# Hybrid decoder block on one core: the output projection in slab pairs with seven-product multiplication, and a new order of steps in all slab pairs

## The chip, the core and the metric

The kernel runs on one core of one Trainium2 chip. The metric is the device time in microseconds. An execution of the kernel before takes 1348.54 us, the median of 3 runs (1348.43 to 1349.02).

## The reference

All values are float32, 256 tokens of width 2048. After an RMSNorm one large projection feeds two attention branches and two sets of gates; then

```python
mixed = g_a * (y_a @ w_branch_a[l]) + g_b * (y_b @ w_branch_b[l])
h = h + mixed @ w_out[l]                                   # 2048 x 2048

hn = rmsnorm(h, ffn_norm[l])
h = h + (jax.nn.silu(hn @ w_gate[l]) * (hn @ w_up[l])) @ w_down[l]   # 2048 x 5632 twice, 5632 x 2048
return rmsnorm(h, final_norm)
```

The change touches this last part, from `mixed` on.

## The kernel before, in words

**Products in three passes.** Each float32 operand is split into a high part in the type float32r and the low rest. A product is hi*hi + lo*hi + hi*lo, all summed in one PSUM accumulator. Activations (128 rows each of two row blocks t = 0, 1) are the stationary operand, weights the moving one, 512 columns wide. A weight tile `raw` (4 times 128 rows by 512 columns, 1 MB) arrives by a DMA that SP issues (`load`, line 904). Six such tiles exist, four of one pool and two of another. `split` (line 916) makes from half a tile the high part `wh` on ScalarE (line 927) and the low part `wl` on VectorE (line 928), each 128 x 1024. It frees the tile after its last use and issues the next load.

**Steps.** All work is written out by hand as a list of steps, and the loop at line 1003 walks it. A plain step takes half a weight tile against both row blocks: 12 matmuls (line 1026 for the passes with `wh`, line 1031 for the pass with `wl`, which comes last). At step s the split of step s + 3 is issued first (`AHEAD`, with four buffers each of `wh` and `wl`), then whatever was put off to this step with `later(d, fn)` or `at(job, d, fn)`, then the step's matmuls. Every engine works through its own queue in the order of issue.

**Jobs.** A job takes one slab of 512 output columns over all chunks of 512 rows of the weight; a plain job of w_out has 8 steps. A pair takes two slabs at once (`pair_steps`, line 832): gate and up columns together for 11 pairs gu0 to gu10, two w_down slabs together for dn0 and dn1. Here the tiles are named (x, c): slab x = 0 or 1 (a and b in the change), chunk c. In two chunks r0, r1 and two slabs the pair replaces eight block products by seven (Winograd's form), each of two steps of 6 matmuls. With A11, A12 the first row block of the two chunks and A21, A22 the second:

- VectorE changes the four weight tiles in place by four subtractions (line 843): T1 = (1, r0) - (0, r0); T2 = (1, r1) - T1; T3 = T2 - (0, r0); T4 = (0, r1) - T2. Each is 128 x 2048 and is issued as `pre` of a split, ahead of its cast.
- The activations give row sums (`row_sums`, line 221): S1 = A21 + A22, S2 = S1 - A11, S3 = A11 - A21, S4 = A12 - S2, four additions on VectorE, then two casts and two subtractions for their high and low parts.
- P1 = A11 (0, r0), P2 = A12 (0, r1), P3 = S4 (1, r1), P4 = A22 T4, P5 = S1 T1, P6 = S2 T2, P7 = S3 T3. They go to four accumulators "11", "21", "12", "22" (row block, slab); all four PSUM buffers of that pool are in use by one pair. `alone` (line 678) copies four intermediate states to SBUF tiles A and B.

In the kernel before the two chunks are 0 and 1 for every pair, and a pair's 22 steps are P1, a20, P5, P2, a22, P3, P6, a30, P4, P7, a32, then b20, b22, b30, b32 (a20: slab a, chunk 2, first half; each P is two steps). T1 goes ahead of P1, T2 of P2, T3 of P3, T4 of P6. The other chunks of w_down follow as plain steps.

**Around the pairs.** `cut` (line 214) splits a transposed chunk into high and low parts. In w_out's jobs, `wout_done` (line 638) adds an accumulator to the residual `xt`, sums its squares on ScalarE (line 166), scales the rows to `hr` (line 654), has TensorE transpose them (line 207), and cuts them: chunk c of the next operand `hop`. The row sums of `hop` are made after slab 1, in the w_out stage. In a gu pair, `gate` (line 691) empties "11" and "21" and applies Silu near the end of the pair; `up` (line 698) empties "12" and "22" in the first step of the next one, with four VectorE operations; the result is transposed in that next pair's fourth and fifth step. `feed` and `feed_sums` (lines 980 to 990) cut the chunks for w_down and make its row sums, once for each of dn0 and dn1, around the start of dn0 and dn1.

## Time and profile before

| what | value |
|---|---|
| median of 3 runs | 1348.54 us |
| the profiled execution | 1348.63 us |
| its span, first to last instruction | 1346.8 us |
| mean granted TensorE clock | 0.943 of full |
| w_out stage in the trace | about 513 to 607 us |
| gu0 to gu10 | 607 to 1083 us |
| dn0, dn1 | 1083 to 1210, 1210 to 1337 us |

The profile is of one execution. Busy times are by engine: PE is TensorE's matmuls, DVE VectorE, ACT ScalarE, SP the engine that issues the loads. A timeline row gives start, duration, engine, line, output <- inputs, and how many instructions were merged; in brackets stands idle time before it and what ended it. Ends of matmuls are modelled.

### The profile page before, as it was taken

How to read it: one execution, taken by the hardware profiler on the slowest of the kernel's cores; microseconds unless marked ns; L12 is line 12 of the kernel's file. 1: busy time of each engine (PE TensorE's matmuls, PEld its weight loads, DVE VectorE, ACT ScalarE, POOL GpSimd, SP SyncE). 2: the span in 40 equal slices, each digit the busy share in tenths (PEclk: the TensorE clock that was granted, in tenths of full speed). 3: DMA queues.
4: the chain of work that ended last, by engine and by line, in shares of the span. 5: the costliest groups of instructions: out<-in, count | busy, mean ns of one | idle time of the engine just before them, and what ended most of it. 6: DMA issues, size and time to landing. Idle time of an engine off the chain costs nothing.

```text
span 1346.8 us, 15873 instructions
## 1 busy us (share of the span) xinstructions
PE 1305.4 (97%) x5990; PEld 1081.8 (80%) x5990; DVE 993.2 (74%) x1212; ACT 782.8 (58%) x1000; POOL 2.1 (0%) x11
## 2 busy tenths in 40 slices
PE   8999999999999999998999999999999989998997
PEld 6888888888888888776887878778787868886885
DVE  5766667674565565578888998889888997579654
ACT  6455555654444454656666666667666665446553
POOL 0000000000000000000000000000000000000000
PEclk9999999999999999999999999999999989998998
DMA  8565544455555565543557545674457637553731
GB/s 295 187 205 182 164 159 153 160 174 189 187 183 160 190 244 188 188 157 118 173 209 250 191 151 185 223 249 156 159 186 249 220 124 250 190 185 108 267 125 63
DMA packets 126969, 249.06 MB, mean 185 GB/s; under 512 B 4486, under 2 KB 9132, under 8 KB 126892
## 3 DMA queue, kind: packets, MB, share of 16 engines
q1 hardware_dynamic: 126620, 247.78, 54.8%
q8 instruction: 47, 0.77, 0.2%
q10 hardware_dynamic: 272, 0.26, 0.1%
q14 instruction: 30, 0.25, 0.1%
HBM read 245.93 MB, written 2.10 MB: 184 GB/s over the span
## 4 chain that ended last, share of the span: by engine, by line
PE 92%; DVE 5%; ACT 2%; issue 1%; DMA 0%; ACTq 0%; SPq 0%; DVEq 0%
PE acc L1026 58%; PE acc L1031 29%; DVE wl L928 2%; DVE raw L843 1%; PE aT_tp L207 1%; ACT wh L927 1%; PE sb L435 1%; ACT junk L166 1%; PE ya L471 0%; PE yb L471 0%; DMA x<-in_x_dram 0%; PE sa L435 0%; PE hT_tp L207 0%; PE xT_tp L183 0%; ACT hr L654 0%
## 5 line engine op out<-in xcount | busy, mean ns | idle before, releaser
L928 DVE TENSOR_TENSOR wl<-raw,wh 128x1024 fp32r<-128x1024 f32 (+2 forms) x546 | 649.2, 1211 | 289.7 <-ACT wh L927 265.8
L927 ACT CAST wh<-raw 128x1024 fp32r<-128x1024 f32 (+2 forms) x546 | 568.1, 1044 | 406.0 <-PE acc L1026 359.6
L1026 PE MATMUL acc<-wh,xh 128*128 128x512 f32 (+1 forms) x512 | 139.4, 394 | 0.0
L1026 PE MATMUL acc<-wh,xl 128*128 128x512 f32 (+1 forms) x512 | 135.5, 387 | 0.0
L1031 PE MATMUL acc<-wl,xh 128*128 128x512 f32 (+1 forms) x512 | 135.3, 386 | 0.0
L843 DVE TENSOR_TENSOR raw<-raw,raw 128x2048 f32<-128x2048 f32 x52 | 118.8, 2285 | 0.4
L1026 PEld LDWEIGHTS acc<-wh,xl 128*128 128x128 f32 x512 | 95.7, 189 | 19.7
L1031 PEld LDWEIGHTS acc<-wl,xh 128*128 128x128 f32 x512 | 95.7, 189 | 19.3
L1026 PEld LDWEIGHTS acc<-wh,xh 128*128 128x128 f32 x512 | 92.0, 190 | 15.2
L1026 PE MATMUL acc<-wh,h2h 128*128 128x512 f32 x176 | 47.1, 390 | 0.0
L1031 PE MATMUL acc<-wl,h2h 128*128 128x512 f32 x176 | 47.1, 389 | 0.0
L1026 PE MATMUL acc<-wh,h3h 128*128 128x512 f32 x176 | 47.1, 389 | 0.0
L1026 PE MATMUL acc<-wh,h2l 128*128 128x512 f32 x176 | 47.0, 389 | 0.0
L1026 PE MATMUL acc<-wh,h3l 128*128 128x512 f32 x176 | 47.0, 389 | 0.0
L1031 PE MATMUL acc<-wl,h3h 128*128 128x512 f32 x176 | 47.0, 389 | 0.0
L1026 PEld LDWEIGHTS acc<-wh,h3h 128*128 128x128 f32 x176 | 33.0, 188 | 6.9
L1031 PEld LDWEIGHTS acc<-wl,h2h 128*128 128x128 f32 x176 | 33.0, 188 | 6.9
L1026 PEld LDWEIGHTS acc<-wh,h3l 128*128 128x128 f32 x176 | 33.0, 188 | 6.9
L1026 PEld LDWEIGHTS acc<-wh,h2l 128*128 128x128 f32 x176 | 33.0, 188 | 6.9
L1031 PEld LDWEIGHTS acc<-wl,h3h 128*128 128x128 f32 x176 | 33.0, 188 | 6.9
L1026 PEld LDWEIGHTS acc<-wh,h2h 128*128 128x128 f32 x176 | 33.0, 188 | 6.8
L1031 PE MATMUL acc<-wl,hq0h 128*128 128x512 f32 x88 | 28.5, 405 | 9.4 <-DVE wl L928 9.4
(444 smaller groups left out, 2013.8 us busy)
## 6 DMA issues: line engine op xcount, KB each, us to landing
raw<-in_w_in_dram SPq DMA_DIRECT2D x59, 1024.0 KB, 5.1
raw<-in_w_gate_dram SPq DMA_DIRECT2D x44, 1024.0 KB, 6.9
raw<-in_w_up_dram SPq DMA_DIRECT2D x44, 1024.0 KB, 5.3
raw<-in_w_down_dram SPq DMA_DIRECT2D x44, 1024.0 KB, 5.2
...
```

The source lines that it names most:

```text
L166: nc.scalar.activation(junk[:, :src.shape[-1]], src, AF.Square, accum_out=acc)
L207: nc.tensor.transpose(tp[:, k, t * P:(t + 1) * P], nat[:, t, (j + k) * P:(j + k + 1) * P], ident)
L435: nc.tensor.matmul(ps[:, t, :], lhsT=l, rhs=r, start=i == 0, stop=i == len(mm) - 1)
L843: sub = lambda o, x, y: (lambda: nc.vector.tensor_sub(raws[G[o]], raws[G[x]], raws[G[y]]))
L927: nc.scalar.copy(hi, v)
L928: nc.vector.tensor_sub(lo, v, f32(hi))
L1026: nc.tensor.matmul(accs[key], lhsT=lhs(k)[i], rhs=hi[:, k], start=i == 0 and k == 0 and jb["first"][key] == s, stop=False, skip_group_chec ...
L1031: nc.tensor.matmul(accs[key], lhsT=lhs(k)[0], rhs=lo[:, k], start=False, stop=(st["read"] or jb["last"][key] == s) and k == 1, skip_group_ ...
```

## The change

The four jobs of w_out become two pairs, wo0 and wo1, each with seven products. The order of a pair's steps is now given by a text, one word per step or product: PLAIN_FIRST for wo0 and gu0, BETWEEN for wo1 and gu1 to gu10, DOWN for dn0 and dn1. The seven products use chunks 2 and 3 (w_out, gate/up) or 3 and 4 (w_down). T2 and T3 are both issued ahead of P6's first half, T4 ahead of its second half. The transposed chunks 2 and 3 of `mixed` are copied to SBUF and cut, and their row sums made; those of `hop` are made from chunks 2 and 3, in gu0; those of w_down's operand once, in dn0, and kept with the cuts of chunks 3 and 4 for dn1. The put-off distances of the residual's leaving change, the Sqrt is issued one step after its inputs, and the multiplication by the final gains is one operation, three steps later.

```diff
+PLAIN_FIRST = "a00 a02 a10 a12 1 2 5 6 3 4 7 b00 b02 b10 b12"
+BETWEEN = "1 a00 2 5 a02 6 3 a10 4 7 a12 b00 b02 b10 b12"
+DOWN = "a00 a02 a10 a12 a20 a22 1 2 a50 5 6 a52 3 4 7 b00 b02 b10 b12 b20 b22 b50 b52"
...
-            nc.scalar.activation(t, v, AF.Sqrt)
+            if apart:
+                later(1, lambda: nc.scalar.activation(t, v, AF.Sqrt))
+            else:
+                nc.scalar.activation(t, v, AF.Sqrt)
...
-            mh.append(big([P, 4, S], f"mh{c}", F32R))
-            ml.append(big([P, 4, S], f"ml{c}", F32R))
-            spread(2, b, mh[c], ml[c], f"mT{c}")
+            if c >= 2:
+                mF[c] = big([P, 4, S], f"mF{c}")
+                for i in range(2):
+                    later(2 + i, lambda i=i: turned(b, mF[c], f"mT{c}", 2 * i))
+
+                def ready():
+                    mop[c] = cut(mF[c], f"m{c}")
+                    if c == 3:
+                        mop["s"], add, finish = row_sums(mF[2], mF[3], "m")
+                        later(1, add)
+                        later(2, finish)
+                later(4, ready)
+            else:
+                mop[c] = [big([P, 4, S], f"m{c}{x}", F32R) for x in "hl"]
+                spread(2, b, *mop[c], f"mT{c}")
...
-    def wout_done(c):
-
-        def done(ps):
...
+    def h_leaves(c, ps, keys):
+
+        h = xt[c]
+        for t in range(NT):
+            nc.vector.tensor_add(h[:, t], ps[keys[t]], h[:, t])
+            sumsq(h[:, t], ssh[:, t, c:c + 1])
+        d, e = ((8, 4), (8, 4), (1, 2), (1, 1))[c]
+        if c == 0:
+            later(2, h0_root)
+            later(5, h0_invert)
+        st = {}
...
-                nc.vector.tensor_add(h[:, t], ps[t], h[:, t])
-                sumsq(h[:, t], ssh[:, t, c:c + 1])
-            d = 4 if c == 0 else 1
-            if c == 0:
-                later(1, h0_root)
-                later(3, h0_invert)
-            st = {}
...
-            def ready():
-                hop[c] = cut(hF[c], f"h{c}")
-                if c == 1:
-                    hop["s"], add, finish = row_sums(hF[0], hF[1], "h")
-                    later(1, add)
-                    later(2, finish)
-            later(d, rows)
-            for i in range(2):
-                later(d + 1 + i, lambda i=i: turned(st["n"], hF[c], f"hT{c}", 2 * i, "ffn", 4 * c))
-            later(d + 3, ready)
...
+        def ready():
+            hop[c] = cut(hF[c], f"h{c}")
             if c == 3:
-                later(3, h_root)
-                later(5, h_invert)
-
-                def both():
-                    v = L["h0_v"]
-                    nc.vector.tensor_mul(hs, v, R["h0"])
-                    nc.vector.tensor_mul(hs, hs, R["h"])
-                later(6, both)
-        return done
+                hop["s"], add, finish = row_sums(hF[2], hF[3], "h")
+                later(1, add)
+                later(2, finish)
+        later(d, rows)
+        for i in range(2):
+            later(d + e + i, lambda i=i: turned(st["n"], hF[c], f"hT{c}", 2 * i, "ffn", 4 * c))
+        later(d + e + 2, ready)
+        if c == 3:
+            later(1, h_root)
+            later(4, h_invert)
+
+            def both():
+                nc.vector.tensor_mul(hs, L["h0_v"], R["h0"])
+                nc.vector.tensor_mul(hs, hs, R["h"])
+            later(5, both)
...
+    def to_residual(jb, j, name):
+
+        A, B = big([P, NT, 512], f"{name}A{j}"), big([P, NT, 512], f"{name}B{j}")
+        alone(jb, A, B)
+        for i, x in enumerate((A, B)):
+            later(jb["pos"]["P7"] + 1 + i, lambda i=i, x=x: nc.vector.tensor_add(xt[2 * j + i], xt[2 * j + i], x))
+
+    def wout_begin(j):
+        def begin(jb):
+            ps, pos = jb["accs"], jb["pos"]
+            to_residual(jb, j, "wo")
+            later(pos["a"] + 1, lambda: h_leaves(2 * j, ps, ("11", "21")))
+            later(pos["b"], lambda: h_leaves(2 * j + 1, ps, ("12", "22")))
+        return begin
...
-            A, B = big([P, NT, 512], f"dA{j}"), big([P, NT, 512], f"dB{j}")
-            alone(jb, A, B)
-            for i, x in enumerate((A, B)):
-                later(pos["P7"] + 3 + i, lambda i=i, x=x: nc.vector.tensor_add(xt[2 * j + i], xt[2 * j + i], x))
+            to_residual(jb, j, "dn")
...
             def leave(i):
                 h = xt[2 * j + i]
                 for t in range(NT):
                     nc.vector.tensor_add(h[:, t], ps[("11", "21", "12", "22")[2 * i + t]], h[:, t])
                     sumsq(h[:, t], ssf[:, t, 2 * j + i:2 * j + i + 1])
-                    nc.vector.tensor_mul(h[:, t], h[:, t], L["gf"][j][:, i])
+                later(3, lambda: nc.vector.tensor_mul(h, h, L["gf"][j][:, i, None, :].to_broadcast([P, NT, 512])))
             if j == 0:
                 later(pos["a"], lambda: leave(0))
                 later(pos["b"], lambda: leave(1))
...
-    for c in range(4):
-        job(w_out[:, 512 * c:512 * (c + 1)], 16, lhs_of(mh, ml), wout_done(c), f"wo{c}")
+    slabs = lambda w, j: [w[:, 512 * c:512 * (c + 1)] for c in (2 * j, 2 * j + 1)]
+    for j in range(2):
+        pair(slabs(w_out, j), 16, mop, wout_begin(j), f"wo{j}", (2, 3), (PLAIN_FIRST, BETWEEN)[j])
     for c in range(11):
-        pair((w_gate[:, 512 * c:512 * (c + 1)], w_up[:, 512 * c:512 * (c + 1)]), 16, hop, gu_begin(c), f"gu{c}")
+        pair((w_gate[:, 512 * c:512 * (c + 1)], w_up[:, 512 * c:512 * (c + 1)]), 16, hop, gu_begin(c), f"gu{c}",
+             (2, 3), BETWEEN if c else PLAIN_FIRST)
     for j in range(2):
-        pair([w_down[:, 512 * c:512 * (c + 1)] for c in (2 * j, 2 * j + 1)], 44, aop, dn_begin(j), f"dn{j}")
+        pair(slabs(w_down, j), 44, aop, dn_begin(j), f"dn{j}", (3, 4), DOWN)
...
-        wa, wb = jb["w"]
+        order = jb["order"].split()
+        r0, r1 = jb["region"]
+        done = max([r1] + [int(u[1]) for u in order if u[0] in "ab"]) + 1
+        for u in order:
+            for x, c in {"1": ((0, r0), (1, r0)), "2": ((0, r1), (1, r1))}.get(u, (("ab".find(u[0]), int(u[-2:-1] or 0)),)):
+                if x >= 0:
+                    get(x, c)
+        for c in range(done, n):
+            get(0, c)
+            get(1, c)
...
-        get((0, 0), (1, 0), (0, 2), (0, 1), (1, 1), (0, 3), (1, 2), (1, 3), *[(x, c) for c in range(4, n) for x in range(2)])
-
-        def seven(name, key, src, lhs, pre=None):
-            for k0 in (0, 2):
-                add_step(jb, G[src], k0, [(key, lhs(k0))], pre if k0 == 0 else None, name)
+        def seven(name, key, src, lhs, *pre):
+            for k0, before in zip((0, 2), (*pre, None, None)):
+                add_step(jb, G[src], k0, [(key, lhs(k0))], before, name)
...
-        seven("P1", "22", (0, 0), A(0, 0), sub((1, 0), (1, 0), (0, 0)))
-        eight(0, 2, 0)
-        seven("P5", "12", (1, 0), S_(1))
-        seven("P2", "11", (0, 1), A(1, 0), sub((1, 0), (1, 1), (1, 0)))
-        eight(0, 2, 2)
-        seven("P3", "12", (1, 1), S_(4), sub((0, 0), (1, 0), (0, 0)))
-        seven("P6", "22", (1, 0), S_(2), sub((0, 1), (0, 1), (1, 0)))
-        eight(0, 3, 0)
-        seven("P4", "21", (0, 1), A(1, 1))
-        seven("P7", "22", (0, 0), S_(3))
-        eight(0, 3, 2, "a")
-        for c in (2, 3):
-            for k0 in (0, 2):
-                eight(1, c, k0, "b")
-        for c in range(4, n):
+        T1, T2 = sub((1, r0), (1, r0), (0, r0)), sub((1, r0), (1, r1), (1, r0))
+        T3, T4 = sub((0, r0), (1, r0), (0, r0)), sub((0, r1), (0, r1), (1, r0))
+        products = {"1": ("22", (0, r0), A(r0, 0), T1), "2": ("11", (0, r1), A(r1, 0)), "5": ("12", (1, r0), S_(1)),
+                    "6": ("22", (1, r0), S_(2), lambda: (T2(), T3()), T4), "3": ("12", (1, r1), S_(4)),
+                    "4": ("21", (0, r1), A(r1, 1)), "7": ("22", (0, r0), S_(3))}
+        for u in order:
+            if u in products:
+                seven("P" + u, *products[u])
+            else:
+                eight("ab".index(u[0]), int(u[1]), int(u[2]), u[0])
+        for c in range(done, n):
             for x, k0 in ((0, 0), (0, 2), (1, 0), (1, 2)) if c == n - 1 else ((0, 0), (1, 0), (0, 2), (1, 2)):
                 eight(x, c, k0, "ab"[x])
+        jb["pos"]["a"] = max(jb["pos"][u] for u in ("a", "P2", "P4", "P7"))
...
-    def feed_sums(j):
-        def go():
-            aop["s"], add, finish = row_sums(aF[0], aF[1], f"d{j}")
-            add()
-            later(2, finish)
-        return go
+    def feed_sums():
+        aop["s"], add, finish = row_sums(aF[3], aF[4], "d")
+        add()
+        later(2, finish)
 
     for j in range(2):
-        at(f"dn{j}", -6, feed(j, 0))
-        at(f"dn{j}", -5, feed_sums(j))
-        at(f"dn{j}", -2, feed(j, 2))
-        at(f"dn{j}", -1, feed(j, 1))
-        at(f"dn{j}", 8, feed(j, 3))
-        for c in range(4, 11):
-            at(f"dn{j}", 22 + 4 * (c - 4) - 4, feed(j, c))
-    at("dn0", 0, load_gfin)
+        at(f"dn{j}", -4, feed(j, 0))
+        at(f"dn{j}", -2, feed(j, 1))
+        at(f"dn{j}", 0, feed(j, 2))
+        at(f"dn{j}", 7, feed(j, 5))
+        for c in range(6, 11):
+            at(f"dn{j}", 30 + 4 * (c - 6) - 4, feed(j, c))
+    for i in range(2):
+        at("dn0", 1 + i, feed(0, 3 + i))
+    at("dn0", 3, feed_sums)
+    at("dn0", 30, load_gfin)
```

## Rows read from the trace of the kernel before

**Rows 1.** The page's busy time by engine: us, share of the span, instructions.

```profile
PE 1305.4 (97%) x5990; PEld 1081.8 (80%) x5990; DVE 993.2 (74%) x1212; ACT 782.8 (58%) x1000; POOL 2.1 (0%) x11
```

**Rows 2.** TensorE's waits: who waited for whom, us in total, times, longest.

```profile
PE acc L1031 <- DVE wl L928: 12.3, 14, 1.7
```

**Rows 3.** Timeline of TensorE in the w_out stage: start, us, what, merged count.

```profile
580.24 1.07 PE L1026 MATMUL acc<-wh,mh 128*128 128x512 f32 x4
...
582.96 1.07 PE L1026 MATMUL acc<-wh,mh 128*128 128x512 f32 x4
...
586.52 0.33 PE L207 MATMUL hT_tp<-ident,hr 128*128 128x128 f32 x1 [0.68 <-ACT hr L654]
...
587.44 1.18 PE L1026 MATMUL acc<-wh,mh 128*128 128x512 f32 x4
```

**Rows 4.** Timeline of TensorE in gu2.

```profile
697.89 0.61 PE L1026 MATMUL acc<-wh,h0h 128*128 128x512 f32 x2
...
703.70 0.71 PE L1026 MATMUL acc<-wh,hq0h 128*128 128x512 f32 x2
...
717.00 0.73 PE L1031 MATMUL acc<-wl,hq0h 128*128 128x512 f32 x2 [0.78 <-DVE wl L928]
```

**Rows 5.** Timeline of VectorE in gu2.

```profile
699.54 0.68 DVE L700 TENSOR_TENSOR up<-acc,up 128x512 f32<-128x512 f32 x1
...
702.19 1.22 DVE L928 TENSOR_TENSOR wl<-raw,wh 128x1024 fp32r<-128x1024 f32 x1
703.44 2.29 DVE L843 TENSOR_TENSOR raw<-raw,raw 128x2048 f32<-128x2048 f32 x1
705.65 3.49 DVE L928 TENSOR_TENSOR wl<-raw,wh 128x1024 fp32r<-128x1024 f32 x3
```

**Rows 6.** Timeline of ScalarE in the w_out stage and in gu2.

```profile
538.98 1.28 ACT L152 ACT_TABLE_LOAD   x1
...
559.28 0.63 ACT L166 ACTIVATE junk<-x 128x512 bf16<-128x512 f32 x1 [2.84 <-DVE x L643]
...
704.91 1.05 ACT L927 CAST wh<-raw 128x1024 fp32r<-128x1024 f32 x1 [0.33 <-PE acc L1026]
```

**Rows 7.** Timeline of TensorE in gu0.

```profile
607.10 0.62 PE L1026 MATMUL acc<-wh,h0h 128*128 128x512 f32 x2
...
610.66 0.33 PE L207 MATMUL hT_tp<-ident,hr 128*128 128x128 f32 x1 [2.04 <-ACT hr L654]
...
621.65 1.07 PE L1026 MATMUL acc<-wh,h2h 128*128 128x512 f32 x4
...
626.60 0.73 PE L1031 MATMUL acc<-wl,hq1h 128*128 128x512 f32 x2 [1.15 <-DVE wl L928]
...
631.34 0.73 PE L1031 MATMUL acc<-wl,hq0h 128*128 128x512 f32 x2 [1.68 <-DVE wl L928]
```

**Rows 8.** Timeline of TensorE where dn0 and dn1 begin.

```profile
1083.29 0.62 PE L1026 MATMUL acc<-wh,d_0h 128*128 128x512 f32 x2
...
1092.53 1.65 PE L1026 MATMUL acc<-wh,d_2h 128*128 128x512 f32 x3 [4.18 <-DVE up L700]
...
1097.39 1.03 PE L207 MATMUL aT_tp<-ident,ga 128*128 128x128 f32 x4
...
1106.92 0.61 PE L1026 MATMUL acc<-wh,d0q1h 128*128 128x512 f32 x2
...
1210.58 0.70 PE L1026 MATMUL acc<-wh,d_0h 128*128 128x512 f32 x2
...
1232.09 0.62 PE L1026 MATMUL acc<-wh,d1q1h 128*128 128x512 f32 x2
...
1237.14 0.73 PE L1031 MATMUL acc<-wl,d1q0h 128*128 128x512 f32 x2 [1.27 <-DVE wl L928]
```

**Rows 9.** Windows: length, TensorE busy, granted clock, DMA share, GB/s.

```profile
608.00:610.00 2.00, 0.62 (x3) 0.95 0.00 0
...
1092.00:1094.00 2.00, 1.47 (x4) 0.50 0.00 0
```

More of the change, by code (lines that the diff above doesn't have):

```diff
@@ L142, in block_kernel, with rstd @@
     L = {}
[L145 removed]
+    def rstd(ss, n, name, apart=False):
         v, r, t = [const([P, NT], name + x) for x in ("_v", "", "_t")]
@@ L318, in job, with pair @@
         jobs.append(dict(w=w, kt=kt, n=w.shape[1], lhs=lhs, done=done, name=name))
-    def pair(w, kt, ops, begin, name):
-        jobs.append(dict(w=w, kt=kt, ops=ops, begin=begin, name=name))
+    def pair(w, kt, ops, begin, name, region, order):
+        jobs.append(dict(w=w, kt=kt, ops=ops, begin=begin, name=name, region=region, order=order))
     later_q = {}
@@ L617, in wb_done @@
         return done
-    mh, ml = [], []
+    mF, mop = {}, {}
     hop, hF, aF, aop = {}, {}, {}, {}
@@ L622, in block_kernel @@
     ssf = const([P, NT, 4], "ssf")
-    R["h"], h_root, h_invert = rstd(ssh, D, "rstd_h")
-    R["h0"], h0_root, h0_invert = rstd(ssh[:, :, 0:1], 512, "rstd_h0")
+    R["h"], h_root, h_invert = rstd(ssh, D, "rstd_h", True)
+    R["h0"], h0_root, h0_invert = rstd(ssh[:, :, 0:1], 512, "rstd_h0", True)
     hs = const([P, NT], "hs")
@@ new lines, in wa_done, with rows @@
+        return done
+    def h_leaves(c, ps, keys):
[8 more added lines that the diff above has]
+        st = {}
+        def rows():
+            st["n"] = big([P, NT, 512], f"hr{c}")
+            for t in range(NT):
+                nc.scalar.mul(st["n"][:, t], h[:, t], R["h0"][:, t:t + 1])
+            hF[c] = big([P, 4, S], f"hF{c}")
+        def ready():
+            hop[c] = cut(hF[c], f"h{c}")
+            if c == 3:
+                hop["s"], add, finish = row_sums(hF[2], hF[3], "h")
[12 more added lines that the diff above has]
+            later(5, both)
@@ L835, in pair_steps, with get @@
         ops, n = jb["ops"], jb["kt"] // 4
-        wa, wb = jb["w"]
+        order = jb["order"].split()
+        r0, r1 = jb["region"]
+        done = max([r1] + [int(u[1]) for u in order if u[0] in "ab"]) + 1
         G = {}
-        def get(*cs):
-            for x, c in cs:
-                G[x, c] = add_group((wa, wb)[x], 4 * c, 4)
+        def get(x, c):
+            if (x, c) not in G:
+                G[x, c] = add_group(jb["w"][x], 4 * c, 4)
+        for u in order:
[5 more added lines that the diff above has]
+            get(1, c)
         sub = lambda o, x, y: (lambda: nc.vector.tensor_sub(raws[G[o]], raws[G[x]], raws[G[y]]))
-        get((0, 0), (1, 0), (0, 2), (0, 1), (1, 1), (0, 3), (1, 2), (1, 3), *[(x, c) for c in range(4, n) for x in range(2)])
-        def seven(name, key, src, lhs, pre=None):
-            for k0 in (0, 2):
-                add_step(jb, G[src], k0, [(key, lhs(k0))], pre if k0 == 0 else None, name)
+        def seven(name, key, src, lhs, *pre):
+            for k0, before in zip((0, 2), (*pre, None, None)):
+                add_step(jb, G[src], k0, [(key, lhs(k0))], before, name)
         def eight(x, c, k0, tag=None):
```

7 lines of the change are left out of this document (removed).

## The prediction

> **What bounds the kernel now.** I read the page first, then the waits of TensorE, then its timeline around each wait. TensorE is busy 97% of the span [rows 1], so only two things can pay: fewer matmuls, or less of the 41 us (1346.8 - 1305.4) in which no matmul runs. The waits [rows 2] say that VectorE's low parts (`wl`, line 928) make it wait 14 times for 12.3 us, the largest sum by far. The timelines place the stops: two in the w_out stage, where transposes wait for `hr` [rows 3], one in each gate/up pair [rows 4], and clusters where gu0, dn0 and dn1 begin [rows 7, 8]. Elsewhere matmuls run back to back: a plain step of 12 takes 582.96 - 580.24 = 2.72 us [rows 3], so one matmul costs 0.227 us and a step of a seven (6 matmuls) 1.36.
>
> VectorE's price list: a low part occupies 1.22 us, 1.14 in a back-to-back row (3.49 for three) [rows 5]; the in-place subtraction of two weight tiles (T1 to T4) 2.2 (703.44 to 705.65) [rows 5]; the four additions that make row sums some 2.5, by the 512-column operation of 0.68 [rows 5]. A cut of an operand chunk has a low part's shape, so 1.14. A seven thus needs 1.14 of VectorE for 1.36 of TensorE, and four subtractions per pair come on top. VectorE can't bank work: the cast of step s+3 starts only when the matmuls of step s-1 have left its buffer, two thirds through that step: the cast of 704.91 waits for the step that TensorE began at 703.70 [rows 4, 6]. So I count, from the last point where VectorE is caught up, its queue up to the low part of P6's second half (P6b), the last that a subtraction delays, and compare that with when TensorE, unstopped, would read it (0.9 us into that step).
>
> **The parts.**
>
> *Matmuls.* Per w_out pair, two chunks of two slabs take 7 x 12 matmuls for 96: 12 fewer, 24 in all, x 0.227 = **-5.4 us**. This is certain.
>
> *w_out pair 0* (plain steps first). Three plain steps and two transposes (0.47 each) put step 3 at 9.1 us; P2b's cast can start at 11.1 and ends at 12.2. Then VectorE has five low parts (P2b, P5a, P5b, P6a, P6b) 5.7, two lows of the row sums 2.3, the sums 2.5, T2 to T4 6.6: it ends at 29.3. TensorE would read at 11.8 + 7 x 1.36 + 0.9 = 22.2. **+7.1.** T1 and the cut of chunk 3 are hidden in the plain steps, where VectorE has 2.72 us per low part.
>
> *w_out pair 1* (BETWEEN). Its start collides with the leaving of pair 0. Counted from its first matmul, VectorE ends b12 at -8.9 (its cast may begin two thirds through P7b, at -11.1); T1, P1a, the addition of A (1.14, by its width) and two accumulator additions (1.35, as `up`'s of 0.68) follow to -3.1; P1b waits for its cast, which stands behind two Squares on ScalarE (0.63 and a read of 0.2 each [rows 6]), and ends at -0.1; the addition of B, a00, the reduction for the root and P2a end at 3.7, the second slab's additions at 5.0. ScalarE squares until 5.9 and then loads the table for the first Sqrt, 1.28 [rows 6], and P2b's cast behind it ends at 8.4. P2b, P5a, the inversion (0.9), P5b, a02, T2, T3, P6a, T4, P6b end at 22.9; TensorE would read at 15.9. **+7.0.**
>
> *The `hr` stops.* After the transposes of 586.52 the main matmuls resume at 587.44, 1.76 us after the step's end (582.96 + 2.72), against 0.4 for undisturbed transposes; the same at 562 [rows 3]. The new delays (rows 8 steps, transposes 12 steps after leaving) remove both: **-2.7**.
>
> *gu0* (plain first, but its sums are now made here and not under w_out). `hr` of slab 3 stands on ScalarE behind Squares, a cast and copies and ends near 8.6, though TensorE is there at 6.4; that puts step 3 at 12.25, and P2b's cast, two thirds on, ends at 15.3. Then five low parts 5.7, three cuts 3.4, inversion and hs 1.2, sums 2.5, T2 to T4 6.6 reach 34.7. TensorE, unstopped: 4 transposes 1.9, 4 plain 10.9, seven steps 9.5, 0.9 = 23.2. Late 11.5. Today's gu0 loses 14.55 - 11.7 = 2.85 up to the end of P2, and 1.15 + 1.68 plus restarts 0.2 after [rows 7]: 5.9. **+5.6.**
>
> *gu1 to gu10* (BETWEEN). The start is as now: the four `up` operations run from 1.65 to 4.3 us into the pair [rows 4, 5]. Then three low parts to 7.7; a02's cast, as now, ends at 8.1; a02 9.2, T2 and T3 13.6, P6a 14.8, T4 17.0, P6b 18.2. TensorE: five pairs of steps 13.6, transposes 0.9, P6a 1.36, 0.9 = 16.8. Late 1.4. Today T2 comes earlier and P6a is late by 0.93 (idle 0.78 plus the modelled tail) [rows 4]. Ten times 0.49: **+4.9**. VectorE is busy without a break from `up` to P6 in both orders; the new one has one low part less (1.14) ahead of a read that comes 1.36 earlier, and leaves VectorE 0.4 idle before a02.
>
> *dn0.* Six plain steps take away the stop of 4.2 us, in which a20 waits for an accumulator that `up`, behind cuts and sums, has not emptied [rows 8]: the first steps now take the two that `gate` has emptied. VectorE is saturated from 1.0: 12 low parts 13.7, six cuts 6.8, `up` 2.65, four subtractions 8.8, sums 2.5, to 35.5; TensorE would read at 30.4. Late 5.1, against 23.6 - 14.5 = 9.1 now. **-4.0.**
>
> *dn1.* No sums, fewer cuts, and the multiplication no longer makes VectorE wait for Squares. VectorE is caught up at P1: a50's cast ends 2.15 after it, then six low parts or cuts 6.8 and T2 to T4 6.6 = 15.6, against 13.1. Late 2.5; now 21.5 - 13.6 = 7.9, plus 1.4 at P6 [rows 8], 9.3. **-6.8.**
>
> *At nothing:* SP's queue holds almost only the weight loads; their number stays, and they are issued in the new order of use as tiles come free, six tiles ahead: a pair frees its eight tiles at much the same steps as now, and no wait of TensorE is put down to a weight load now; the copies of chunks 2 and 3 of `m` to SBUF replace high-part casts one for one; w_out's additions of A and B lie under its b steps, 1.14 each, except as counted in pair 1. The multiplication of two rows at once isn't in the trace; between one operation of 1024 columns and two of 512 it is 1.1 to 1.4, under plain steps.
>
> Sum: -5.4 + 7.1 + 7.0 - 2.7 + 5.6 + 4.9 - 4.0 - 6.8 = **+5.7**. The profiled execution took 1348.63 us (span 1346.8), the median 1348.54, so 1354.3 and **1354.2 us**.
>
> **The clock.** After the 4.2 us stop in dn0 the granted clock is 0.50, its 1.2 GHz level, and 12 matmuls and their transposes take 2.7 us more than at 0.95 (the 2.4 GHz level) [rows 8, 9]; with a 2.04 us stop in gu0 it stays at 0.95 [rows 7, 9]. The new stops in pair 0 and gu0 are split into pieces of 1 to 2.7 us, nearer to the second row, so I take no fall; the bounds are 0 and 2.7 for each of the two places. The Trainium skill ("TensorE: Matmul & The Clock Gate", section "HAM oscillation — how this bites in real kernels") says that a matmul kernel whose bursts are parted by long waits falls to the low level again and again, each burst starting cold; by that rule the sum would be +11.1. The trace agrees at dn0 and not at gu0.
>
> **Rivals.**
> 1. *VectorE's bunches cost no more than today's.* If the queue recovers within each bunch, as it does in today's gu0 (3.05 of lateness for the same four subtractions), then w_out 0 and 1, gu0 and dn0 cost 3.05 each, the pairs after gu0 nothing, and dn1 as counted: -5.4 + 6.1 - 2.7 - 2.85 - 6.05 - 6.8 = -17.7, **1330.8**. For it: T's operands are there early. Against it: today's gu0 has its sums made beforehand, and its VectorE has no idle time left where it stops. It decides if P6b's lateness in pair 0 is under 4.
> 2. *About even.* T2 to T4 find gaps in the BETWEEN pairs (0 for 4.9) and the table load falls under other work (3.3 for 7.0, the queue without the 3.7 us in which it waits for P2b's cast): -2.9, **1345.6**. For it: only half a microsecond per pair separates the orders.
> 3. *The clock falls* in pair 0 and gu0: +11.1, **1359.6**, by the row at dn0.
>
> **How the numbers follow.** Forecast 0.45, its own range 1350 to 1358; rival 1 0.20; rival 2 0.20; rival 3 0.15. A difference of 0.2% (2.7 us) is about what can be measured. Rival 2 lies astride the bound: 0.10 faster, 0.10 the same; of the forecast 0.05 is the same. So faster 0.30, same 0.15, slower 0.55. The range takes in the forecast, rivals 2 and 3 with their errors of 2 to 4 us, and a little of the way to rival 1: 1339 to 1361.
>
> **What would show it.** Right: TensorE waits for `wl` of P6 in every pair, 1.4 (printed near 1.2) in gu1 to gu10; 5 us or more of stops between P5 and P6b in w_out 0 and in gu0; a wait for `wh` at P2b of w_out 1 with a table load before it; no 4 us wait for an accumulator at dn0 or dn1; 360 matmuls with `m` operands for 384. Wrong: the pairs' period falls to 42.0 from 42.8, or VectorE shows idle time ahead of P6 in w_out 0.

## The result and the profile after

The changed kernel takes 1360.62 us (four runs, 1359.46 to 1361.61) beside 1348.49 us for the one before on the same chip: 12.1 us slower, ratio 1.0091, 95% interval 1.0073 to 1.0108. Forecast was +5.7 (1354.2), so the direction held and the size forecast was half of what came. The profiled execution took 1359.46 us, its span is 1357.3.

Page of the changed kernel: busy time by engine, to set beside [rows 1].

```profile
PE 1302.5 (96%) x5966; PEld 1073.4 (79%) x5966; DVE 1026.2 (76%) x1230; ACT 793.9 (58%) x1020; POOL 2.1 (0%) x11
```

The 24 fewer matmuls are there (5990 - 5966). VectorE has 33 us more work.

Its waits of TensorE: who waited for whom, us in total, times, longest; the first answers to [rows 2].

```profile
PE acc L1066 <- DVE wl L963: 24.6, 21, 1.7
...
PE acc L1061 <- ACT dnA L698: 1.9, 2, 0.9
...
PE acc L1061 <- ACT woA L698: 0.9, 1, 0.9
PE acc L1061 <- ACT ga L698: 0.9, 1, 0.9
```

The low parts make TensorE wait twice as long as before. Waits for the copies at line 698 (`alone` copies an accumulator to an SBUF tile) are new: four of them, of 0.9 us each, and no step of the prediction has them. Where it all lies is read from TensorE's timeline: first the two w_out pairs and gu0, then gu1, gu2, dn0, dn1 (start, duration, what, and in brackets the idle time ahead and who ended it).

```profile
536.22 1.22 PE L1061 MATMUL acc<-wh,mq0h 128*128 128x512 f32 x2 [2.75 <-ACT wh L962]
...
541.86 0.99 PE L1066 MATMUL acc<-wl,mq0h 128*128 128x512 f32 x2 [0.41 <-DVE wl L963]
...
550.86 0.39 PE L1061 MATMUL acc<-wh,m0h 128*128 128x512 f32 x1
552.19 0.97 PE L1061 MATMUL acc<-wh,m0h 128*128 128x512 f32 x3 [0.94 <-ACT woA L698]
...
553.91 1.07 PE L1066 MATMUL acc<-wl,m0h 128*128 128x512 f32 x4
554.82 1.07 PE L1061 MATMUL acc<-wh,m0h 128*128 128x512 f32 x4
...
562.98 0.61 PE L1061 MATMUL acc<-wh,m2h 128*128 128x512 f32 x2
...
584.98 0.73 PE L1066 MATMUL acc<-wl,mq0h 128*128 128x512 f32 x2 [1.23 <-DVE wl L963]
...
611.49 0.60 PE L213 MATMUL hT_tp<-ident,hr 128*128 128x128 f32 x4
...
635.88 1.22 PE L1061 MATMUL acc<-wh,hq0l 128*128 128x512 f32 x2 [1.66 <-DVE hq0l L244]
...
646.02 0.73 PE L1066 MATMUL acc<-wl,hq0h 128*128 128x512 f32 x2 [1.68 <-DVE wl L963]
...
666.87 0.61 PE L1061 MATMUL acc<-wh,h2h 128*128 128x512 f32 x2
...
728.74 0.73 PE L1066 MATMUL acc<-wl,hq0h 128*128 128x512 f32 x2 [1.41 <-DVE wl L963]
...
772.20 0.73 PE L1066 MATMUL acc<-wl,hq0h 128*128 128x512 f32 x2 [1.41 <-DVE wl L963]
...
1101.55 1.07 PE L1061 MATMUL acc<-wh,d_0h 128*128 128x512 f32 x4
...
1137.40 0.73 PE L1066 MATMUL acc<-wl,dq0h 128*128 128x512 f32 x2 [1.67 <-DVE wl L963]
...
1226.25 1.07 PE L1061 MATMUL acc<-wh,d_0h 128*128 128x512 f32 x4
...
1258.57 0.74 PE L1066 MATMUL acc<-wl,dq0h 128*128 128x512 f32 x2 [1.68 <-DVE wl L963]
```

Stage borders are the first matmul or transpose of a stage. Those of before are 513.34 (w_out), 607.10, 655.03 (gu1), 1083.29 and 1210.58 (three of them in [rows 7, 8]); those of after are 512.13, 611.49, 666.87, 1101.55 and 1226.25.

| stage | before, us | after, us | measured | forecast |
|---|---|---|---|---|
| ahead of w_out | 513.3 | 512.1 | -1.2 | 0 |
| w_out | 93.8 | 99.4 | +5.6 | +6.0 |
| gu0 | 47.9 | 55.4 | +7.5 | +5.6 |
| gu1 to gu10 | 428.3 | 434.7 | +6.4 | +4.9 |
| dn0 | 127.3 | 124.7 | -2.6 | -4.0 |
| dn1 and the end | 136.2 | 131.1 | -5.2 | -6.8 |
| span | 1346.8 | 1357.3 | +10.5 | +5.7 |

The first line is no effect of the change: in seven experiments whose code is that of the changed kernel up to there w_out begins between 512.3 and 513.7. With it the spans differ by 10.5 where the medians differ by 12.1; the profiled execution of the changed kernel is 1.2 below its median. The upper level of TensorE's clock is printed as 0.95 in the profiled execution before and as 1.00 in the one after; the pace is the same, 2.72 us for a plain step (603.33 - 600.61 after).

### The profile page after: what moved, and what is told of

It reads as the page before. It is cut to its first block, busy times and chain, and to the rows that moved or that the text cites. A ratio compares the mean times of both kernels' runs of the same rounds, so it can differ in the third digit from the quotient of the medians.

```text
span 1357.3 us, 15904 instructions
## 1 busy us (share of the span) xinstructions
PE 1302.5 (96%) x5966; PEld 1073.4 (79%) x5966; DVE 1026.2 (76%) x1230; ACT 793.9 (58%) x1020; POOL 2.1 (0%) x11
## 4 chain that ended last, share of the span: by engine, by line
PE 82%; DVE 9%; issue 6%; ACT 3%; DMA 0%; DVEq 0%; ACTq 0%; SPq 0%
PE acc L1061 52%; PE acc L1066 26%; DVE wl L963 4%; DVE raw L883 4%; ACT wh L962 2%; PE sb L441 1%; ACT junk L172 0%; PE ya L477 0%; PE yb L477 0%; PE aT_tp L213 0%; DMA x<-in_x_dram 0%; PE sa L441 0%; PE xT_tp L189 0%; PE pTa L464 0%; PE pTb L464 0%
## 5 line engine op out<-in xcount | busy, mean ns | idle before, releaser
L1061 PE MATMUL acc<-wh,h0h 128*128 128x512 f32 x176 | 47.5, 391 | 0.9 <-ACT ga L698 0.9
L1061 PE MATMUL acc<-wh,h1h 128*128 128x512 f32 x176 | 47.2, 390 | 0.0
L1066 PE MATMUL acc<-wl,h0h 128*128 128x512 f32 x176 | 47.1, 389 | 0.0
L1061 PE MATMUL acc<-wh,h0l 128*128 128x512 f32 x176 | 47.1, 389 | 0.0
L1061 PE MATMUL acc<-wh,h1l 128*128 128x512 f32 x176 | 47.0, 389 | 0.0
L1066 PE MATMUL acc<-wl,h1h 128*128 128x512 f32 x176 | 47.0, 389 | 0.0
L1061 PEld LDWEIGHTS acc<-wh,h0l 128*128 128x128 f32 x176 | 33.0, 188 | 6.9
L1066 PEld LDWEIGHTS acc<-wl,h0h 128*128 128x128 f32 x176 | 33.0, 188 | 6.9
L1061 PEld LDWEIGHTS acc<-wh,h1l 128*128 128x128 f32 x176 | 33.0, 188 | 6.9
L1066 PEld LDWEIGHTS acc<-wl,h1h 128*128 128x128 f32 x176 | 33.0, 188 | 6.9
```

Source lines behind the costliest of these rows:

```text
L1061: nc.tensor.matmul(accs[key], lhsT=lhs(k)[i], rhs=hi[:, k], start=i == 0 and k == 0 and jb["first"][key] == s, stop=False, skip_group_chec ...
L1066: nc.tensor.matmul(accs[key], lhsT=lhs(k)[0], rhs=lo[:, k], start=False, stop=(st["read"] or jb["last"][key] == s) and k == 1, skip_group_ ...
```

## The experiments

All are medians of four or five runs, with kernels of one group beside the same runs of the kernel before (1347.6 to 1348.3; beside the changed kernel it took 1348.5). A difference between two groups can hold up to 0.9 us of that shift. "Less" and "more" are against the changed kernel where nothing else is said. Theory A throughout is the prediction's: what counts is VectorE's queue up to the low part that TensorE reads next.

**1. The old order in gu1 to gu10.** Chunks 2 and 3 stay; the subtractions T2, T3, T4 are at P2, P3 and P6 as before.

```
+OLD = "1 a00 5 2 a02 3 6 a10 4 7 a12 b00 b02 b10 b12"
...
-(2, 3), BETWEEN if c else PLAIN_FIRST)
+(2, 3), OLD if c else PLAIN_FIRST)
...
+products.update({"2": (..., T2), "3": (..., T3), "6": (..., T4)})
```

> Only gate/up pairs 1 to 10 differ from the changed kernel: the product order and the places of the four subtractions are those of before, the seven products still use chunks 2 and 3. Theory A (the subtractions crowd VectorE ahead of P6's second half, because P3's two steps now stand behind it): the pair period goes from 43.46 back to 42.83, ten times 0.63, so the total falls by 6.3 us to about 1354.3, and the stop at P6's second half (1.41 us) becomes the 0.78 us stop at its first half. Rival B (it is the later chunks, their loads and their place among the gate and up work, not the order): the period stays near 43.4 and the total near 1360.6.

Measured 1354.6 (ratio 1.0045, 1.0032 to 1.0059): 6.0 us less. The timeline of TensorE has the stop of before again.

```profile
730.71 0.73 PE L1070 MATMUL acc<-wl,hq0h 128*128 128x512 f32 x2 [0.79 <-DVE wl L967]
773.53 0.73 PE L1070 MATMUL acc<-wl,hq0h 128*128 128x512 f32 x2 [0.77 <-DVE wl L967]
```

The period is 42.82 (773.53 - 730.71) for 43.46 (772.20 - 728.74). The kernel before had 42.83. So the whole loss of these ten pairs is the order of steps and subtractions; the later chunks cost nothing.

**2. Two subtractions at the products that need them** (BETWEEN pairs; the tile (1, r0) is kept until P7).

```
-"6": (..., lambda: (T2(), T3()), T4), "4": (...), "7": (...)
+"6": (..., T2), "4": (..., T4), "7": (..., T3)
```

> In the second w_out pair and gate/up pairs 1 to 10 two of the three subtractions at P6 go to the products that need them: the one for P4 ahead of P4, the one for P7 ahead of P7; the buffer they read is held until then. Theory A (the bunch ahead of P6's second half costs the time): the 1.41 us stop goes from every pair, period 42.0 to 42.1, ten times 1.4 is 14 us, and 2 to 3 us of the second w_out pair's 3.3 us of stops: total 1343 to 1346. Rival B (VectorE has no slack in the seven products as a whole, so the lateness only moves to P4 or P7): period 43.2 to 43.5 with a wait for wl at P4 or P7, total 1357 to 1361. Rival C (the held buffer delays a load): waits for a raw tile at b00 or b10, total above 1361.

Measured 1388.87 (1.0304, 1.0290 to 1.0319), worse than every rival. The stop at P6 is gone, but a wait of 2.36 us for the high part has come at P7; TensorE's timeline:

```profile
747.78 0.73 PE L1071 MATMUL acc<-wh,hq1h 128*128 128x512 f32 x2 [2.36 <-ACT wh L970]
```

VectorE's timeline ahead of P4 of the same pair:

```profile
738.23 2.28 DVE L883 TENSOR_TENSOR raw<-raw,raw 128x2048 f32<-128x2048 f32 x1
741.71 1.23 DVE L971 TENSOR_TENSOR wl<-raw,wh 128x1024 fp32r<-128x1024 f32 x1 [1.20 <-ACT wh L970]
```

ScalarE's:

```profile
740.63 1.05 ACT L970 CAST wh<-raw 128x1024 fp32r<-128x1024 f32 x1 [3.84 <-DVE raw L883]
```

The subtraction writes the very tile that is split next. ScalarE can cast it only after 740.5, and VectorE, whose next instruction is the low part of that cast, stands idle for 1.20 us. Three engine steps that overlapped before now follow each other, three times in each pair (1.20 us each ahead of P6 and P4, 1.19 ahead of P7). In the changed kernel T3, behind T2, fills this gap. By stages 20 us are lost in gu0 to gu10, 7 in w_out and 1.9 in dn0, where the granted clock fell in this execution. The period is 44.85, and longer (45.8 to 46.4) four times, where TensorE falls to half pace (granted clock 0.50 from 839 to 841).

**3. Each subtraction ahead of a step that does not read it** (BETWEEN pairs; (1, r0) is kept until a10).

```
-"6": (..., lambda: (T2(), T3()), T4)
+"6": (..., None, T4)
+early, keep = {"a02": T2, "a10": T3}, "a10"
```

> As the changed kernel, but in the second w_out pair and gate/up pairs 1 to 10 each subtraction stands ahead of a step that does not read it: P6's source ahead of the plain step before P6, P7's source ahead of the plain step behind P3 (the buffer held until then), P4's source ahead of P6's second half as in the change. Theory A (the stop at P6's second half is the sum of VectorE's queue ahead of it; one subtraction of 2.3 us less there is more than the 1.41 us it is late): the stop goes, period 42.0 to 42.2, total 1360.6 - 13 to 16 = 1345 to 1348. Rival B (the sum over all seven products is what does not fit, lateness moves to the plain step or P4): 43.2 to 43.5 and 1358 to 1361. Rival C (as in the run with subtractions at P4 and P7: VectorE idles 1.2 us behind each subtraction for ScalarE's copy of the same tile): 1370 or more.

Measured 1342.74 (0.9962, 0.9949 to 0.9974): 17.9 us less, more than the forecast 13 to 16. TensorE's timeline, the first matmul of two pairs:

```profile
708.04 0.62 PE L1071 MATMUL acc<-wh,h2h 128*128 128x512 f32 x2
...
749.79 0.62 PE L1071 MATMUL acc<-wh,h2h 128*128 128x512 f32 x2
```

No stop is left in gu1 to gu10 (three, of 0.27 to 0.90, are left in the second w_out pair) and the period is 41.75. It fell by 1.71 (43.46 - 41.75) for a printed stop of 1.41: **a stop costs 0.3 us more than its printed length**. The rows around the stop at 728.74 show where the 0.3 lies: ahead of it two matmuls are printed as 0.62 long though the next two start 0.45 later (726.27 and 726.72), and behind the stop the next two start only 0.57 later (729.31). With one subtraction (2.28 us) less ahead of P6's second half the stop is gone; VectorE's total work is the same. T2 also goes one step earlier here; experiment 9 moves a single subtraction.

**4. Down's part alone**, on the kernel before: the diff's hunks for it.

```
-pair([w_down[...] for c in (2 * j, 2 * j + 1)], 44, aop, dn_begin(j), f"dn{j}")
+pair(slabs(w_down, j), 44, aop, dn_begin(j), f"dn{j}", (3, 4), DOWN)
...
+at("dn0", 3, feed_sums)
```

> The kernel before with the down projections' part of the change alone: its order (six plain steps first, chunks 3 and 4 in the seven products), row sums made once, the feeds and adds at their new places; w_out plain, gate/up as before. Theory A (the stages are additive; down gained 2.3 and 5.5 us in the changed kernel): 1348.5 - 7.8 = 1340.7. Rival B (the terms of the prediction, 4.0 and 6.8, hold and the rest was lost to the other stages): 1337.7. Rival C (the gain of down in the changed kernel is only what its late gate/up pairs left over): within 2 us of 1348.5.

Measured 1340.95 (0.9950, 0.9937 to 0.9962), as theory A said. The stages add up: the change holds a gain of about 7 us, and w_out with gate/up loses 19.

**5. w_out as four plain jobs in the changed kernel.**

```
-pair(slabs(w_out, j), 16, mop, wout_begin(j), f"wo{j}", (2, 3), (PLAIN_FIRST, BETWEEN)[j])
+job(w_out[:, 512 * c:512 * (c + 1)], 16, lhs_of(mh, ml), wout_done(c), f"wo{c}")
```

> The changed kernel with w_out as four plain jobs as before; gate/up (later chunks, plain steps first in its first pair, the new order) and down as changed. Theory A (the stages add up: the two w_out stages took 5.6 us more than before, the first gate/up pair lost its own 7.2 us by the row sums that it makes just before their use): 1360.6 - 4.4 to 5.6 = 1355 to 1356.2, the first gate/up pair 54 to 55.5 us long. Rival B (the first gate/up pair is late because the w_out pairs hand over two slabs of h at their end): its stops at P5 and P6 go as well, 1347 to 1350, that pair 48 to 50 us long.

Measured 1353.93 (1.0037, 1.0025 to 1.0050): the w_out pairs cost 6.7 us. gu0 still makes its sums just before their use, and now has the same stop as the first w_out pair had; this is its timeline of TensorE.

```profile
633.74 1.22 PE L1044 MATMUL acc<-wh,hq0h 128*128 128x512 f32 x2 [2.75 <-ACT wh L945]
```

gu0 takes 53.4 us here (607.17 to 660.61), 1.9 less than after: that much of its loss comes from the pairs' late slabs, the rest is its own. Theory A, though its forecast for the total was 1 to 2 us too high.

**6. The w_out pairs and down with gate/up as before**, gu0's order too; so the row sums of `hop` are again made from chunks 0 and 1, in w_out.

```
-(2, 3), BETWEEN if c else PLAIN_FIRST)
+(0, 1), OLD)
```

> The changed kernel with gate/up back to the kernel before (chunks 0 and 1 in the seven products, its order and its subtraction places, the first pair too); w_out in pairs and down as changed. Against the run with down alone (1340.95) it differs by w_out alone. Theory A (the w_out pairs cost more in stops than their 24 fewer matmul pairs save: the two stages took 99.4 us for 93.8): 1340.95 + 4.4 to 5.6, that is 1345.4 to 1346.6, with the half-clock stretch at P6 of the first pair. Rival B (w_out itself gains its 5.4 us of matmuls and the first gate/up pair carries the loss): 1336 to 1341.

Measured 1357.24 (1.0071, 1.0058 to 1.0084): both theories fall, the w_out pairs cost 16 us beside the run with down alone, 10.4 of them in w_out. TensorE's timeline has two stops that neither kernel has.

```profile
604.59 1.29 PE L1065 MATMUL acc<-wh,m0h 128*128 128x512 f32 x3 [2.69 <-ACT woA L699]
...
626.16 1.51 PE L214 MATMUL hT_tp<-ident,hr 128*128 128x128 f32 x4 [4.73 <-ACT hr L672]
```

At the first the copy of P7's accumulator stands on ScalarE's queue behind the casts of the row sums, which wait for VectorE's additions; ScalarE's timeline:

```profile
600.86 1.06 ACT L244 CAST hq0h<-hq 128x1024 fp32r<-128x1024 f32 x1 [2.04 <-DVE hq L238]
```

The second is one of order: a pair hands over two slabs at its end, and the old gu0 wants the last ones (chunks 2 and 3) from its third step on. This run suggests that the plain steps at the head of gu0 are no free choice but what w_out in pairs requires, and that their bunch belongs to the price of w_out; only this one other order was run without them.

**7. The first pairs spread.**

```
-PLAIN_FIRST = "a00 a02 a10 a12 1 2 5 6 3 4 7 b00 b02 b10 b12"
+PLAIN_FIRST = "a00 a02 a10 1 2 a12 5 3 6 4 7 b00 b02 b10 b12"
+products.update({"3": (..., T2), "6": (..., None, T4), "4": (..., T3)})
```

> As the changed kernel, but in the first w_out and first gate/up pair one plain step stands between P2 and P5, P3 stands ahead of P6, and one subtraction goes behind P6 (ahead of P4). Theory A (the stops at P6 bring the half-clock stretch of 5.5 us with them, in both places): the stops ahead of P6 shrink from 2.75 and from 1.9 + 1.7 to under 1.5, no matmul at half pace, and the two stages lose 3 to 4 us of stops and 2.9 us of half pace each: total lower by 8 to 11, 1350 to 1353. Rival B (the half clock comes by itself at these places, or by the row-sum waits that stay): lower by 2 to 5, 1355.5 to 1358.5, with matmuls at 1.05 us per two still there.

Measured 1363.4 (1.0115, 1.0101 to 1.0128), 2.8 more: neither theory. The stop ahead of P6 is gone, a larger one is where P3 follows P5; TensorE's timeline:

```profile
537.35 1.22 PE L1072 MATMUL acc<-wh,mq1h 128*128 128x512 f32 x2 [4.18 <-ACT woB L698]
```

ScalarE's:

```profile
534.82 1.99 ACT L971 CAST wh<-raw 128x1024 fp32r<-128x1024 f32 x2 [3.05 <-DVE raw L883]
536.71 0.58 ACT L698 COPY woB<-acc 128x512 f32<-128x512 f32 x1
```

P5 and P3 use the same accumulator ("12"), and between them ScalarE must copy P5's product out. The copy stands on its queue behind casts that wait 3.05 us for a subtraction. Whether shorter stops avoid the half pace stayed untested, since the stop didn't get shorter.

**8. b00 behind P7.** First the four high-part matmuls of the free accumulator ahead of those of the one being copied, at the four places where b00 follows P7:

```
+in_turn = "begin" in jb and steps[s - 1]["tag"] == "P7" and st["tag"] == "b"
```

> Where a plain b step follows P7 directly (first w_out pair, first gate/up pair, both down pairs) the matmuls of its first accumulator all come first and those of the accumulator that ScalarE is still copying come after them: 4 matmuls of hi weights, 0.9 us. Theory A (the 0.94 us stops at those four places are the wait for ScalarE's copy of P7's accumulator): the stops fall to 0 to 0.1, total lower by 3.5 to 5 us, 1355.6 to 1357. Rival B (the wait is hidden behind something else at these places, or the copy itself waits for later work): total within 1 us of 1360.6.

Measured 1360.34 (1.0087, 1.0073 to 1.0101). The four stops shrank from 0.94 to 0.26 each, but the 2.7 us that this makes did not come: the wait ahead of a00 in the second w_out pair grew from 0.34 to 0.76, and in this execution dn0 fell to half pace from 1135.5 on, where the changed kernel did not, and was 1.2 us longer. The total decides between neither theory. Then all six matmuls of the free accumulator first:

```
+for mm in ([m] for m in st["mm"]) if apart else (st["mm"],):
```

> As the changed kernel, but in the b00 step that follows P7 directly (first w_out pair, first gate/up pair, both down pairs) all six matmuls of the free accumulator, low parts too, come before the six of the accumulator that ScalarE copies: 1.36 us of cover for 0.94 us, where the run before gave 0.9. Theory A (each of the four stops costs 1.24 us, 0.94 printed and 0.3 of restart; together the 5.0 us that the prediction left out): no wait for a copy at these places, 1355 to 1356.5; by stages 1.2 us less in each of the four, where no half-pace stretch falls otherwise. Rival B (the copy's wait only takes the place of VectorE's or ScalarE's lateness in the steps behind it): stops of the same size in b02 or b10, 1359.5 to 1361.

Measured 1358.98 (1.0077, 1.0064 to 1.0091), 1.6 less. No wait for a copy is left; TensorE's timeline in the first w_out pair and behind it:

```profile
552.20 0.61 PE L1063 MATMUL acc<-wh,m0h 128*128 128x512 f32 x2
...
555.02 1.07 PE L1063 MATMUL acc<-wh,m0h 128*128 128x512 f32 x4
...
567.61 0.97 PE L1063 MATMUL acc<-wh,m0h 128*128 128x512 f32 x3 [1.32 <-DVE x L660]
```

By stages gu0, dn0 and dn1 are each 1.1 us shorter (54.3, 123.6, and 119.6 for 120.8 from dn1's first matmul to the start of the last group) and the first w_out pair 1.0. The second gives that back: its a00 now waits 1.32 us for an accumulator that waited 0.34 before. So a copy stop costs what its rows say (the two high-part groups of b00 take 3.05 us from 550.86 to 553.91 after, against 1.81 for the next two from 554.82, which are undisturbed: 1.24), three of four come back, and the next wait takes the fourth. That is 3.3 us by stages for the 5.0 that theory A gave; the medians show 1.6, less than their own spread of 3, so the total alone shows nothing here and the stages carry the proof.

**9. One subtraction later on top of down alone.** Down alone as in 4, and T3 of every gate/up pair moved from P3 to the plain step behind P6:

```
-"3": (..., T3)
+early, keep = {"a30": T3}, "a30"
```

> The kernel before with down's part alone (1340.95), and in all gate/up pairs P7's subtraction moved from P3 to the plain step behind P6, its buffer held one step longer. Theory A (the 0.78 us stop at P6's first half of every pair is VectorE's queue there; one subtraction less ahead of it removes it): period 42.83 to 42.05 to 42.1, eleven times 0.75, total 1332 to 1334. Rival B (VectorE's sum over the pair sets the period; the stop moves behind P6): 1339 to 1341.

Measured 1328.99 (0.9862, 0.9847 to 0.9877): 12.0 us less than down alone, the 0.78 us stop of [rows 4] is gone and the period is again 41.75 (11 x 1.08 = 11.9, the stop and its 0.3). This is TensorE's timeline, the first matmul of two pairs.

```profile
695.85 0.61 PE L1054 MATMUL acc<-wh,h0h 128*128 128x512 f32 x2
...
737.60 0.61 PE L1054 MATMUL acc<-wh,h0h 128*128 128x512 f32 x2
```

More than forecast by 3 to 5 us, of which the 0.3 at each of eleven stops makes 3.3. On top of it down's order, and b00 as in the first edit of 8:

```
-DOWN = "a00 a02 a10 a12 a20 a22 1 2 a50 5 6 a52 3 4 7 b00 ..."
+DOWN = "a00 a02 a10 a12 1 2 a20 a22 5 a50 6 3 4 a52 7 b00 ..."
+"6": (..., None, T4), "4": (..., T3), early = {"a50": T2}
```

> The run with down alone and the gate/up subtraction one step later (1328.99), and in both down pairs: four plain steps ahead of the seven products and four among them, each subtraction ahead of a plain step or a product that does not read it, one of them behind P6; and the matmuls of b00's first accumulator all ahead of those of the second. Theory A (each stop costs its length and 0.31 us more, as the 0.78 us stop did, whose end shortened the gate/up pair by 1.09; down's stops print 5.2 us in the first pair in five places and 3.3 us in the second in three): 8.5 + 8 x 0.31 = 11.0 us are there to be had, 9 to 10.5 come: 1318.5 to 1320. Rival B (VectorE's sum over the seven products with the row sums does not fit into their time, so lateness moves to P4 or P7): 3 to 5 us come, 1324 to 1326, with a wait for wl or wh at P4 or P7.

Measured **1323.82** (0.9818, 0.9804 to 0.9831), 5.2 less than the run before it. dn1 lost 3.6 us, all it had but a 0.26 us stop; dn0, where VectorE also makes the row sums and cuts five chunks, only 1.3: it has stops of 0.62, 0.67, 1.15 and 0.26 and, as rival B said, a new one of 1.23 for `wl` at P4 (at 1110.14). Theory A for dn1, B for dn0; for the total it is B.

**10. w_out's middle slabs as one pair**, on top of that:

```
+pair([w_out[:, 512 * i:512 * (i + 1)] for i in (1, 2)], 16, mop, wout_begin, "wo1", (2, 3), OLD23)
```

> The run before this with w_out's slabs 1 and 2 as one pair with the seven products (chunks 2 and 3, the order and the subtraction places of the gate/up pairs of that run), slab 0 ahead of it and slab 3 behind it as plain jobs. Theory A (the seven products gain their matmuls, 12 x 0.227 = 2.7 us, where row sums and operands are there long before and plain steps stand between): that run less 1.5 to 3 us, no wait for wl or wh in the pair over 0.3 us. Rival B (two slabs that leave together bring VectorE and ScalarE a bunch, hr and the row sums of h come late): equal to that run or up to 3 us above it, with waits for hr in slab 3 or the first gate/up pair.

Measured 1330.25 (0.9865, 0.9851 to 0.9878), worse by 6.4, mainly for one stop and a stretch at half pace behind it (granted clock 0.50 from 549 to 552); TensorE's timeline:

```profile
548.79 1.51 PE L210 MATMUL hT_tp<-ident,hr 128*128 128x128 f32 x4 [6.33 <-ACT hr L669]
```

VectorE's timeline shows the subtraction and the last operation of the inversion that `hr` waited for:

```profile
543.69 2.29 DVE L885 TENSOR_TENSOR raw<-raw,raw 128x2048 f32<-128x2048 f32 x1
...
547.82 0.16 DVE L162 TENSOR_TENSOR rstd_h<-rstd_h,rstd_h_t 128x2 f32<-128x2 f32 x1
```

Work that is set some steps later comes twice as early where the steps are sevens. With later steps for slab 0:

```
-later(1, h0_root), later(3, h0_invert), d = 4
+later(2, h0_root), later(5, h0_invert), d, e = 8, 4
```

> As the run with w_out's slabs 1 and 2 in one pair (1330.25), but slab 0's square root, inversion, scaling and turning are set for later steps (2, 5, 8, 12 for 1, 3, 4, 5), because a step of the seven products is half as long. Theory A (the 6.33 us stop before slab 0's turning, for a scaling that waited for an inversion behind a 2.3 us subtraction on VectorE, and the 4 us at half pace behind it were the only loss): 6.3 + 0.3 + 2.3 less, 1321 to 1322, that is 2 to 3 us under the run without a w_out pair (1323.82). Rival B (the pair costs its 2.7 us elsewhere, the wait goes to the second turning or the row sums): 1323.5 to 1326.

Measured 1323.72 (0.9819, 0.9805 to 0.9832), the same as without the pair (rival B). The big stop is gone; w_out takes 93.3 us for 93.7, since stops of 0.95 and 0.28 for `wl` in the pair, with 0.3 each, and half a microsecond more of waits for `hr` eat most of the 2.7 us of matmuls. Ahead of the 0.95 VectorE had stood idle for a cast that ScalarE's queue held behind the Squares of slab 0; VectorE's timeline:

```profile
540.75 2.36 DVE L982 TENSOR_TENSOR wl<-raw,wh 128x1024 fp32r<-128x1024 f32 x2 [1.89 <-ACT wh L981]
```

w_out in sevens gained nothing in any form tried.

## Why the prediction had the sign and half the size

**The queue reckoning held.** P6's second half was to be read when VectorE's queue ends. The times count from the start of the stage (in w_out 1 from its first matmul):

| | forecast, us | measured, us |
|---|---|---|
| w_out 0 | 29.3 | 541.86 - 512.13 = 29.7 |
| w_out 1 | 22.9 | 584.98 - 562.98 = 22.0 |
| gu0 | 34.7 | 646.02 - 611.49 = 34.5 |
| dn0 | 35.5 | 1137.40 - 1101.55 = 35.9 |

In w_out 1 the foreseen stop of TensorE at P2b did not come, but its cause did: VectorE stood idle there, since the cast that it waited for stood behind the Squares and the table load, 3.45 us for the forecast 3.7, and TensorE feels it only later. VectorE's timeline, and the table load on ScalarE's:

```profile
570.42 2.36 DVE L963 TENSOR_TENSOR wl<-raw,wh 128x1024 fp32r<-128x1024 f32 x2 [3.45 <-ACT wh L962]
```

```profile
567.95 1.28 ACT L156 ACT_TABLE_LOAD   x1
```

The pair was late by 6.1 (22.0 - 15.9) for the forecast 7.0: its four stops (0.34, 0.98, 1.11, 1.23, and 0.3 each) make 4.9, a transposition and delays too short to be printed the rest.

**The step that failed is "At nothing".** It weighed the copies of chunks to SBUF and the additions of A and B, but left out the copy of P7's accumulator on ScalarE, and so put its wait at nothing without a reason. Before, an a step that doesn't use that accumulator stood between P7 and the first b step. PLAIN_FIRST and DOWN put b00 there. The rows show the wait in four places, 1.24 us each, 5.0 in all, where 6.4 (12.1 - 5.7) is missing. The stages bear this out, once two transpositions of slab 2 (0.47 each) are set right, which went from w_out to gu0 and stand in no term: with them w_out is 0.5 above its forecast and gu0 1.0.

| | above forecast, us | copy stop | queue read, measured less forecast |
|---|---|---|---|
| w_out | 0.5 | 1.24 | 0.4 - 0.9 |
| gu0 | 1.0 | 1.24 | -0.2 |
| dn0 | 1.4 | 1.24 | 0.4 |
| dn1 | 1.6 | 1.24 | 0.4 (from P1, 1258.57 - 1242.57 = 16.0 for 15.6) |

The last two columns add up to the first within 0.3. Experiment 8 brings back 1.0 to 1.1 at each of the four places, though in w_out the next wait takes it again. That w_out came out at +5.6 for +6.0 is luck: the copy stop, the second pair's 0.9 and the moved transpositions cancel.

**The second is the size of the term 10 x 0.49 for gu1 to gu10.** The prediction had a pair late by 1.4 for 0.93. Against a pair without a stop, which experiments 3 and 9 gave, it is 1.71 (43.46 - 41.75) for 1.08 (42.83 - 41.75): 0.63 per pair, 1.4 us more in all. The mechanism, VectorE's queue up to P6, is shown by experiments 1, 3 and 9.

**Rival 3 came out near the time by luck.** The clock did fall in both places it named. Windows of the changed kernel, with length, busy time of PE, PEld, DVE, ACT and POOL, granted clock, DMA share and GB/s:

```profile
537.00:541.00 4.00, 3.77 (x10) 2.29 (x8) 4.00 (x4) 2.71 (x5) 0.00 (x0) 0.50 0.00 0
...
636.00:641.00 5.00, 5.00 (x12) 3.58 (x13) 4.96 (x3) 1.75 (x2) 0.00 (x0) 0.50 0.00 0
```

0.50 is the 1.2 GHz level, as at dn0 before [rows 9]; this is the half pace of the experiments, two matmuls every 0.85 us (539.54 to 540.39) for 0.45. By the rival that is 5.4 us; by the rows it is close to nothing, since VectorE is busy through both windows (4.00 of 4, 4.96 of 5) and TensorE, slow or not, still waits for it afterwards (0.41 at 541.86, 1.68 at 646.02). The two queue ends above are those forecast without a fall. The experiments confirm it for gu0: in 1 and in the first run of 8 its stretch at 0.50 was about half as long, and P6's second half was read 34.5 us from its start all the same. The Trainium skill ("TensorE: Matmul & The Clock Gate", section "HAM oscillation — how this bites in real kernels") says that bursts parted by long waits start cold again; the trace agrees that the level falls there, behind waits of 2.75 us and less, and differs on what that is worth.

**Rivals 1 and 2.** Rival 1 fell by its own sign: P6's second half in w_out 0 was late by 7.5 (29.7 - 22.2), not by under 4. Rival 2 fell with the pair period: VectorE found no gaps, as its idle time in gu2 was 0.30 us ahead of a02 and none between T2 and P6b. Its other half, a table load that falls under other work, failed with the 3.45 us idle in w_out 1. VectorE's timeline in gu2 (the two subtractions at 719.61 are T2 and T3), to set beside [rows 5]:

```profile
718.46 1.23 DVE L963 TENSOR_TENSOR wl<-raw,wh 128x1024 fp32r<-128x1024 f32 x1 [0.30 <-ACT wh L962]
719.61 4.61 DVE L883 TENSOR_TENSOR raw<-raw,raw 128x2048 f32<-128x2048 f32 x2
724.13 1.22 DVE L963 TENSOR_TENSOR wl<-raw,wh 128x1024 fp32r<-128x1024 f32 x1
725.27 2.29 DVE L883 TENSOR_TENSOR raw<-raw,raw 128x2048 f32<-128x2048 f32 x1
727.47 4.62 DVE L963 TENSOR_TENSOR wl<-raw,wh 128x1024 fp32r<-128x1024 f32 x4
```

Open stays why dn0 falls to half pace in some executions and not in others with the same stops, and what the first pairs would cost if their sums were made earlier, which wasn't tried.
